# Two-layer hybrid RWKV-7/GLA block on one core: channel-quarter modulation, fused state update, output part in two passes

## The chip, the cores and the metric

One Trainium2 chip; the program runs on 1 core. The metric is the device time of one execution in microseconds (us). Before the change it is 2909.24 us, the median of 3 runs (2906.11 to 2914.11).

## What is computed

```python
for l in range(2):                                  # x_lat: 512 tokens, x_ctx: 256 tokens, 1024 channels
    mod = silu(c) @ ada_w[l] + ada_b[l]             # shift, scale, gate; latent and context rows
    h = rms_norm(x) * norm_mix_pre * (1 + sc_m) + sh_m
    f = h @ w_in[l]                                 # 44 column tiles of 128
    y_rw  = rwkv7(f)   # S_t = S_{t-1}(diag(w_t) - kk_t^T(a_t kk_t)) + v_t^T k_t, both directions, 8 heads
    y_gla = gla(f)     # S = diag(decay) S + k^T v by chunks of 64, both directions, 4 heads
    m = (g_rw * (y_rw @ rw_out) + g_gla * (y_gla @ gla_out)) @ merge_out
    x = x + g_m * rms_norm(m)
    x = x + g_f * rms_norm(square(relu(modulate(x) @ w1)) @ w2)
# context seeds the latent scans; in the last layer only the latent stream goes on after the scans
```

## The kernel before

Activations lie transposed, channels on partitions: 8 tiles of 128 channels, each 768 columns (256 of context "c", 512 latent "l"; GROUPS cuts the latent into "l" and "l2" of 256). Every float32 operand of a large product is split in a high and a low fp32r part, so a weight tile of 128 x 128 costs three matmuls: high by high, high by low, low by high. In the trace these are d<-sh,wh, d<-sl,wh and d<-sh,wl, of 512 or 256 columns. load_w (line 648) fetches a weight in two halves of 256 KB on the SP queue (wr), ScalarE copies the high part (wh), and GpSimd or VectorE subtracts for the low part (wl).

All instructions are recorded by Order and issued from one place (line 541, so the profile names that line for all). A list scheduler (flush, choose) models the five queues with a cost per instruction and issues each engine's instructions in the order of its plan; it is run five times: start, token mixing 0, output part 0, token mixing 1, output part 1. Numbers in CFG and module constants steer it. On the chip each engine then goes through its queue in that order.

- Start (lines 1907 to 1946): the 8 x tiles come in; sum_sq (789) gets the sums of squares per group; scaled multiplies x by the norm. ada_steps (720) takes 32 pieces of the modulation weights (wa, 256 KB each, 8 channel tiles k by 4 quarters u, k outermost), adds each product to acc on VectorE and, after the last, transposes acc and forms MT (shift) and AB (scale). Only then is x modulated (sh high, sl low), and first_tiles (880) multiplies it by column tiles 12, 13 and 14 of w_in, first l, then c, with the weights loaded for each stream.
- Token mixing (897 to 1771): for 6 units (4 of RWKV, 2 of GLA) and 3 groups of 4 chunks, threads of small matmuls are woven with large products as fill (gates, next projections, ada pieces). rw_C (1297) is the sequential part of RWKV: in each of 4 steps a product with the state ZS (c<-ZS,AR), a copy (pre), a product (c<-pre,YI), a copy (ZA), a product (c<-ZA,TK), and the state update on VectorE. There are 2 x 12 x 4 - 8 = 88 such updates; gla_C (1547) has 44 of its own, on GZ.

```python
dve.tensor_tensor(out=gs[hs], in0=pr[hs, :, h], in1=zs[hs, sl, h, :], op=ALU.add)
dve.tensor_tensor(out=nz[hs, ns, h, :], in0=gs[hs], in1=E[hs, sl]..., op=ALU.mult)   # both for h = 0, 1
```

- Output part (1773 to 1897): merge product (weights wmrg, 8 tiles), norm and residual, MLP with 4 blocks of 8 tiles w1 and 8 tiles w2, norm and residual, and in layer 0 the first tiles of layer 1. post_mod (829) is the norm chain of one group: sum_sq of the product, u and x (multiply and residual add), sum_sq of x, then u, sh and sl, the input of the next product. To give PE work meanwhile, held (1809) keeps the last weights on chip (4 of 8 in layer 0, 5 in layer 1, and 3 of w1) and runs through them once for each group of 256 columns; the other tiles go over 512 and 256 columns at once (body). weave (851) sets at which step a group's chain goes on.

Of the kernel before, what the change touches and what calls it, by code (L numbers as in the profile page):

```python
# [53 lines left out]
def constants():  # L54
# [44 lines left out]

CFG = {  # L100
    "nfill": ((2, 2, 0, 2, 2, 0, 2, 2, 0, 2, 2, 0, 2, 1, 1, 0, 0, 0, 0), (2, 3, 0, 2, 2, 1, 2, 2, 0, 2, 2, 0, 1, 0, 0, 1, 0, 0, 0)),
    "nada": ((2,) * 12 + (0,) * 7, (2,) * 8 + (0,) * 11),
# [13 lines left out]
    "oe": ((-1, 1, 2, 9, 10), (-1, 1, 2, 5, 7)),  # L116
    "ch": (0,),
# [19 lines left out]
LATEF = 50e3  # L137


class Order:  # L140
# [7 lines left out]
    def __init__(self, tc):  # L148
        self.tc = tc
        self.nodes = []  # L150
        self.clock = {e: 0.0 for e in ISSUE}
        self.dma = 0.0
        self.flow, self.win, self.sum, self.slow, self.lost = deque(), 0, 0.0, False, 0.0
        self.cfg = None
        self.table = None
        self.alloc = {}
        self.slots = {}
        self.free0 = 0.0
        self.last = {}
        self.end_of = {}  # L160
        self.serial = {}
# [35 lines left out]
    def add(self, key, op, fn, a, k):  # L197
# [61 lines left out]
        if key == "PE":  # L259
            n["kind"] = (n["cfg"], str(lhs.dtype), op, n["w"][0][0].cap_key if n["w"] else None)  # L260
            n["calls"] = 1
            n["fill"] = bool(n["w"]) and str(n["w"][0][0].cap_key).startswith("d1")
# [54 lines left out]
    def flush(self):  # L317
        self.depend()
        ns = self.nodes
        left, members = {}, {}  # L320
        for n in ns:
# [6 lines left out]
            for name, t in ts.items():  # L328
# [9 lines left out]
                elif left[name] == 1:  # L338
                    kk = self.slots[t.cap_key]
                    kk["free"] = [x for x in kk["free"] if x[1] != name]  # L340
        want, cands = {}, {e: [] for e in ISSUE}
# [34 lines left out]
        def choose(e):  # L376
# [15 lines left out]
            best, low = [], None  # L392
            for n in cands[e]:
# [19 lines left out]
            if e == "PE" and self.cold(low):  # L413
                d = [x for x in best if x[0] <= low + tol and x[1]["flow"] >= 0.7 * x[1]["d"]]
                near = d or near
            return min(near, key=lambda x: x[1]["prio"])
# [9 lines left out]
        while done < len(ns):  # L426
# [11 lines left out]
            if e == "DVE" and n["two"] and self.clock["POOL"] > s + 100.0:  # L438
                d += 0.9 * min(d, self.clock["POOL"] - s)
            f = s + d  # L440
            if e == "POOL" and vec is not None and vec["two"] and self.clock["DVE"] > s + 50.0:
                x = 0.9 * min(self.clock["DVE"] - s, d)
# [17 lines left out]
            if e == "SP":  # L460
                self.dma = max(self.dma, s + 1300.0) + n["bytes"] / 200.0
                f = self.dma + 700.0
# [9 lines left out]
            for name, t in n["tiles"].items():  # L472
# [12 lines left out]
                if not left[name]:  # L485
# [63 lines left out]
def hybrid_kernel(ctx: ExitStack, tc: tile.TileContext, A: dict, out: bass.AP):  # L549
# [96 lines left out]
    D0, D1 = One("d0"), One("d1")  # L646

# [141 lines left out]
    def sum_sq(pl, xs, grp, cuts, eng=pool, psp=ops):  # L789
        s, o, n = grp  # L790
        nt = n // 128
        parts = []
        for j in range(KT):
            x = xs[j][:, o:o + n]
            if j in cuts:
                S = pl.tile([P, n], F32, name="S", tag="S", bufs=6)
                act.activation(out=S, in_=x, func=AF.Square)
                parts.append(S)
            else:
                q = pl.tile([P, n], F32, name="q", tag="q", bufs=2)  # L800
                act.activation(out=q, in_=x, func=AF.Square)
                eng.tensor_tensor(out=parts[-1], in0=parts[-1], in1=q, op=ALU.add)
            if j == 5 and cuts is CHAIN:
                yield
        pc = psp.tile([P, 512], F32, name="d", tag="d")
        for i, S in enumerate(parts):
            for t in range(nt):
                mm(pc[:, t:t + 1], S[:, 128 * t:128 * t + 128], ones, start=(i == 0 and t == 0),
                   stop=(i == len(parts) - 1 and t == nt - 1))
# [19 lines left out]
    def post_mod(pl, ms, l, which, grp, xs, store_x, l2, which2, acts):  # L829
        s, o, n = grp  # L830
        si = SI[s]
        bc = yield from sum_sq(pl, ms, grp, CHAIN)
# [10 lines left out]
        bc = yield from sum_sq(pl, xs, grp, PAIRS)  # L843
# [7 lines left out]
    def weave(dd, dw, chains, offs, then=()):  # L851
# [7 lines left out]
        for p in range(max(len(steps), max(at) + 1)):  # L859
            for ch in at.get(p, ()):  # L860
                next(ch, None)
# [35 lines left out]
    def mixer(l, acts, adas, pre, early):  # L897
# [399 lines left out]
        def rw_C(X, gi):  # L1297
# [10 lines left out]
            for st in range(4):  # L1308
                cc = (st, 7 - st)
                sl = slice(st, 8 - st, 7 - 2 * st)  # L1310
                pp = cps.tile([P, 2, 2, 64], F32, name="c", tag="c")
# [14 lines left out]
                if st < 3:  # L1326
                    nz, ns = zs, slice(st + 1, 7 - st, 5 - 2 * st)
                else:
                    nz, ns = nzs, slice(0, 8, 7)
                pr = cps.tile([P, 2, 2, 64], F32, name="c", tag="c")  # L1330
                gs = G([P, 2, 64], "gs", 2)
# [215 lines left out]
        def gla_C(X, gi):  # L1547
# [9 lines left out]
            for st in range(4):  # L1557
# [11 lines left out]
                sl = slice(st, 8 - st, 7 - 2 * st)  # L1569
                nz, ns = (z, slice(st + 1, 7 - st, 5 - 2 * st)) if st < 3 else (nz_, slice(0, 8, 7))  # L1570
                gs = G([P, 2, 128], "Q", 2, name="gs2")
                for h in range(2):
                    hs = HS[h]
                    dve.tensor_tensor(out=gs[hs], in0=pu[hs, st % 2], in1=z[hs, sl, h, :], op=ALU.add)
                    dve.tensor_tensor(out=nz[hs, ns, h, :], in0=gs[hs], in1=E[hs, sl].unsqueeze(2).to_broadcast([64, 2, 128]), op=ALU.mult)
# [197 lines left out]
    def out_mlp(l, last, ya, wo):  # L1773
        full = l == 0
        st = STREAMS if full else STREAMS[:1]
        groups = GROUPS if full else GROUPS[:2]
# [4 lines left out]
        with ExitStack() as mx:  # L1781
# [4 lines left out]
            nt = 4 if full else 5  # L1786
            hslots = [[(hp, t, 8) for t in ("ah", "al", "ah", "al")]] * (nt - 1) + [None]
            bslots = [None] + [[(bp, t, 8) for t in ("bh", "bl", "bh", "bl")]] * 2
# [20 lines left out]
            def held(srcs, acts, evac, ms_, slots):  # L1809
                ws = {}  # L1810

                def one(i, m, g):
                    if m not in ws:
                        ws[m] = load_w(srcs[m], slots[i], PD)
                    evac(m, dense(ws[m], acts(), [g]), [g])

                return [[(lambda i=i, m=m, g=g: one(i, m, g)) for i, m in enumerate(ms_)] for g in groups]
# [22 lines left out]
            xs = []  # L1840
            for j in range(8):
# [180 lines left out]
```

## Time and profile before

| | |
|---|---|
| median of the runs | 2909.24 us |
| profiled execution | 2908.16 us, span 2906.4 us |
| mean granted TensorE clock | 0.961 |
| PE busy / VectorE / ScalarE / GpSimd | 2714.6 / 1635.9 / 1242.9 / 1128.6 us |
| bytes moved | 257.12 MB, mean 88 GB/s |

PE is TensorE, DVE VectorE, ACT ScalarE, POOL GpSimd, SP the queue that issues the transfers. A busy PE is not PE at its peak: the ends of matmuls are modelled, so the pitch from start to start tells more than the duration. A window row gives each engine's busy time in a stretch and its granted clock.

### The profile page before, as it was taken

What the parts mean: (1) busy time and instruction counts of PE and PEld (TensorE: products, weight loads), DVE (VectorE), ACT (ScalarE), POOL (GpSimd) and SP (SyncE); (2) the same over time, 40 slices, a digit from 0 to 9 for tenths busy, and PEclk for the clock granted to TensorE, in tenths of its full rate; (3) what the DMA queues carried; (4) which work ended last, traced back from release to release, by engine and by line L of the source; (5) the groups of instructions that cost most, each with busy time, mean ns of one, the idle gap of its engine ahead of it and who ended that gap; (6) DMA issues with size and microseconds to landing.
All of it is one profiled execution on the core that took longest, in us unless ns stands there. A gap on an engine that the chain in (4) does not pass through costs nothing.

```text
span 2906.4 us, 56280 instructions
## 1 busy us (share of the span) xinstructions
PE 2714.6 (93%) x22616; PEld 2243.8 (77%) x22616; DVE 1635.9 (56%) x3155; ACT 1242.9 (43%) x2542; POOL 1128.6 (39%) x1310
## 2 busy tenths in 40 slices
PE   6999999999988989999999899989988978899998
PEld 4788778778767988888889666767776756888887
DVE  6577888786677251122224538887878787422223
ACT  3555454545552343323133545545444572443332
POOL 2745444542330442223135546444333241533334
PEclk9999999999999989999999899989978999899999
DMA  6422323231225212222222343222301115223332
GB/s 218 130 87 68 106 76 102 81 106 59 83 85 208 83 37 64 64 62 63 65 62 85 109 146 97 74 89 79 98 16 35 40 49 183 78 84 95 95 97 81
DMA packets 137780, 257.12 MB, mean 88 GB/s; under 512 B 15312, under 2 KB 24272, under 8 KB 137520
## 3 DMA queue, kind: packets, MB, share of 16 engines
q1 hardware_dynamic: 137520, 253.53, 28.0%
q8 instruction: 178, 2.92, 0.4%
q14 instruction: 82, 0.67, 0.1%
HBM read 223.45 MB, written 30.02 MB: 87 GB/s over the span
## 4 chain that ended last, share of the span: by engine, by line
PE 54%; DVE 8%; issue 3%; ACT 3%; POOL 3%; DMA 1%; SPq 0%; POOLq 0%; ACTq 0%; DVEq 0%
PE d L541 45%; PE c L541 4%; PE m L541 3%; PE i L541 2%; DMA g<-odr 1%; PE da L541 1%; DVE lw L541 1%; DVE AR L541 1%; POOL S L541 1%; DVE u L541 1%; DVE ZS L541 1%; POOL wl L541 0%; DVE gs L541 0%; DVE BK L541 0%; DVE g L541 0%
## 5 line engine op out<-in xcount | busy, mean ns | idle before, releaser
L541 PE MATMUL d<-sh,wh 128*128 128x512 f32 (+1 forms) x3304 | 1198.4, 363 | 48.0 <-ACT wh L541 19.2
L541 PE MATMUL d<-sh,wl 128*128 128x512 f32 (+1 forms) x3304 | 1144.0, 346 | 12.3 <-POOL wl L541 9.1
L541 PE MATMUL d<-sl,wh 128*128 128x512 f32 (+1 forms) x3304 | 1145.3, 347 | 4.9 <-POOL sl L541 2.8
L541 PEld LDWEIGHTS d<-sh,wh 128*128 128x128 f32 x3304 | 634.0, 192 | 157.7 <-issue 27.4
L541 POOL TENSOR_TENSOR wl<-wr,wh 128x512 fp32r<-128x512 f32 x319 | 427.4, 1342 | 779.6 <-ACT wh L541 715.6
L541 PEld LDWEIGHTS d<-sh,wl 128*128 128x128 f32 x3304 | 633.8, 192 | 95.6 <-POOL wl L541 13.7
L541 PEld LDWEIGHTS d<-sl,wh 128*128 128x128 f32 x3304 | 635.1, 192 | 70.5 <-DVE sl L541 4.8
L541 ACT ACTIVATE wh<-wr 128x512 fp32r<-128x512 f32 x506 | 313.7, 626 | 477.0 <-PE d L541 380.6
L541 DVE TENSOR_TENSOR wl<-wr,wh 128x512 fp32r<-128x512 f32 x187 | 144.3, 777 | 182.1 <-ACT wh L541 177.0
L541 DVE TENSOR_TENSOR t<-t,d 128x256 f32<-128x256 f32 (+1 forms) x102 | 58.2, 572 | 320.4 <-ACT t L541 320.4
L541 POOL TENSOR_TENSOR sl<-t,sh 128x512 fp32r<-128x512 f32 (+2 forms) x73 | 103.1, 1414 | 220.4 <-ACT sh L541 220.4
L541 DVE TENSOR_TENSOR a<-a,d 128x512 f32<-128x512 f32 (+1 forms) x81 | 44.4, 549 | 219.4 <-PE d L541 219.3
L541 ACT ACTIVATE XY<-i 128x512 f16<-128x512 f32 x192 | 109.2, 594 | 108.0 <-PE i L541 106.2
L541 ACT ACTIVATE t<-d 128x256 f32<-128x256 f32 (+1 forms) x102 | 51.4, 506 | 165.2 <-PE d L541 165.1
L541 POOL TENSOR_TENSOR rn<-rn,C 128x2 f32<-128x2 f32 (+2 forms) x41 | 58.8, 1433 | 150.6 <-DVE rn L541 150.2
L541 POOL TENSOR_TENSOR LTL<-AB,LTB 64x512 f16<-64x512 f32 x48 | 63.4, 1322 | 125.3 <-DVE LTB L541 123.5
L541 PE MATMUL da<-wa,SC 128*32 128x128 f32 x1536 | 86.2, 302 | 21.8 <-DMA wa<-in_ada_dram 15.3
L541 POOL TENSOR_TENSOR S<-S,q 128x256 f32<-128x256 f32 x102 | 77.2, 765 | 70.8 <-ACT q L541 69.8
L541 PEld LDWEIGHTS <-XY 64*64 64x64 f16 x1920 | 66.5, 111 | 46.7 <-issue 34.4
L541 DVE TENSOR_TENSOR Q<-i,MK 128x512 f16<-128x512 f32 x120 | 82.6, 689 | 24.2 <-PE i L541 21.4
L541 ACT ACTIVATE f<-d 128x512 f32<-128x512 f32 (+1 forms) x85 | 54.5, 651 | 88.9 <-PE d L541 68.0
L541 PE MATMUL i<-Q,XY 64*64 64x64 f16 x1920 | 84.1, 199 | 8.4 <-DVE Q L541 5.8
(252 smaller groups left out, 4221.5 us busy)
## 6 DMA issues: line engine op xcount, KB each, us to landing
wr<-in_w_dram SPq DMA_DIRECT2D x256, 256.0 KB, 2.7
wa<-in_ada_dram SPq DMA_DIRECT2D x192, 256.0 KB, 2.7
wr<-in_win_dram SPq DMA_DIRECT2D x186, 256.0 KB, 2.9
wr<-in_wout_dram SPq DMA_DIRECT2D x32, 256.0 KB, 3.8
wr<-in_wmrg_dram SPq DMA_DIRECT2D x32, 256.0 KB, 3.1
gdr<-fg SPq DMA_DIRECT2D x20, 384.0 KB, 2.9
gdr<-fg SPq DMA_DIRECT2D x20, 256.0 KB, 2.0
xi<-in_xt_dram SPq DMA_DIRECT2D x8, 384.0 KB, 6.9
```

Of the source, the lines that this page charges most:

```text
L541: ins = fn(*a, **k).ins
```

## The change

1. Start: the modulation weights are taken with the quarter u outermost, each quarter summed in PSUM over its 8 pieces. After each quarter, the two channel tiles j = u and 4 + u are modulated and their part of the three first products (both streams, weights loaded once) is issued.
2. State update: new = E * (product) + E * (old state). ScalarE forms E * old (zse, ze), VectorE does one scalar_tensor_tensor for each direction and head half.
3. Output part: held is replaced by passes: all 8 tiles of wmrg and of the last w2 block go over l (512 columns) and then, loaded again, over c (in layer 1: l, then l2, 256 each); so do the first 3 (layer 1: 5) tiles of w1. The chains of l and l2 start together after the first pass. Sums of squares are formed in two halves, and their PSUM comes from fixed banks.
4. The scheduler gets other costs, other constants for each of its five runs, and other tables of fill.

```diff
-    "nfill": ((2, 2, 0, 2, 2, 0, 2, 2, 0, ...
+    "nfill": ((2, 2, 0, 3, 1, 0, 3, 1, 0, ...
...
-    "oe": ((-1, 1, 2, 9, 10), (-1, 1, 2, 5, 7)),
-    "ch": (0,),
+    "oe": ((-1, 1, 2, 5, 6), (-1, 1, 2, 5, 6)),
+    "ch": (0, 4),
...
+SEG = [
+    dict(AHEAD=20.0, HOLD=8000.0, HYST=0.0, LATE=80000.0, LATEF=80000.0, SLACK=0.0, WARM=0.45),
...
-                n["d"] = 150.0 + 0.87 * c
+                n["d"] = 175.0 + 0.87 * c + (100.0 if any(isinstance(k.get(x), bass.AP) for x in ("bias", "scale")) and c > 64 else 0.0)
...
+    CB = ({"l": D0, "l2": D0, "c": D1}, {"l": D0, "l2": D1})
...
+                if not (gi == NG - 1 and st == 3):
+                    zse = G([P, 2, 64], "zse", 1)
+                    for d in range(2):
+                        for h in range(2):
+                            act.activation(out=zse[HS[h], d], in_=zs[HS[h], cc[d], h, :], func=AF.Copy, scale=E[HS[h], cc[d]:cc[d] + 1])
...
-                for h in range(2):
-                    hs = HS[h]
-                    dve.tensor_tensor(out=gs[hs], in0=pr[hs, :, h], in1=zs[hs, sl, h, :], op=ALU.add)
-                    dve.tensor_tensor(out=nz[hs, ns, h, :], in0=gs[hs], in1=E[hs, sl].unsqueeze(2).to_broadcast([64, 2, 64]), op=ALU.mult)
+                for d in range(2):
+                    for h in range(2):
+                        hs = HS[h]
+                        dve.scalar_tensor_tensor(out=nz[hs, ns[d], h, :], in0=pr[hs, d, h], scalar=E[hs, cc[d]:cc[d] + 1],
+                                                 in1=zse[hs, d], op0=ALU.mult, op1=ALU.add)
...
-            def held(srcs, acts, evac, ms_, slots):
-                ws = {}
...
+            def passes(srcs, acts, evac, ms_):
+                def one(m, g):
+                    evac(m, dense(load_w(srcs[m], None, PD), acts(), [g]), [g])
+
+                return [[(lambda m=m, g=g: one(m, g)) for m in ms_] for g in groups]
...
-        ag = ada_steps(0, 0, ini, "ra", 28)
...
+        for u in range(4):
+            ps = cps.tile([P, 512], F32, name="da", tag="c")[:, 0:128]
+            for k in range(KT):
+                raw = ini.tile([P, 4, 128], F32, name="ra", tag="ra", bufs=26)
...
+                    mm(ps[32 * g:32 * g + 32, :], SC[:, k, :], raw[:, g], start=(k == 0), stop=(k == KT - 1))
...
+            for j in (u, 4 + u):
...
+            for s, o, n in STREAMS:
+                for i, w in enumerate(ws):
...
+                    for q in range(2):
+                        ah, al = acts[4 * q + u]
```

How the order moves, at three places. PE in the start, from the norm to the first large product (da<-wa and da<-ra are the modulation's pieces, da<-C,acc the transpose, d<-sh the projections). Before:

```order
L541 MATMUL d<-C,rn 128x128 x2
L541 MATMUL da<-wa,SC 32x128 x100
L541 MATMUL da<-C,acc 128x128 x4
L541 MATMUL d<-sh,wh 128x512
L541 MATMUL d<-sl,wh 128x512
L541 MATMUL d<-sh,wl 128x512
```

Now:

```order
L566 MATMUL da<-C,acc 128x128
L566 MATMUL da<-ra,SC 32x128 x12
L566 MATMUL d<-C,rn 128x128 x2
L566 MATMUL da<-ra,SC 32x128 x20
L566 MATMUL da<-C,acc 128x128
L566 MATMUL d<-sh,wh 128x512
L566 MATMUL d<-sl,wh 128x512
L566 MATMUL d<-sh,wl 128x512
```

The first projection stood behind all 128 matmuls of the modulation, and now stands behind 64 of them, with the last 64 in two groups of 32 further down among the projections.

VectorE at the first state update of layer 0. Before:

```order
L541 COPY ZA<-c 64x2x64
L541 TENSOR_TENSOR XY<-i,MK 128x8x64
L541 SCALAR_TENSOR_TENSOR lw<-C,lw 128x260
L541 TENSOR_TENSOR gs<-c,ZS 64x128
L541 TENSOR_TENSOR ZS<-gs,E 64x2x64
L541 TENSOR_TENSOR gs<-c,ZS 64x128
L541 TENSOR_TENSOR ZS<-gs,E 64x2x64
L541 SCALAR_TENSOR_TENSOR lw<-C,lw 128x260
```

Now VectorE, and behind it ScalarE in a later step:

```order
L566 COPY ZA<-c 64x2x64
L566 TENSOR_TENSOR XY<-i,MK 128x8x64
L566 SCALAR_TENSOR_TENSOR ZS<-c,E,zse 64x64 x4
L566 SCALAR_TENSOR_TENSOR ta<-ta,kk 128x256
L566 COPY pre<-c 64x128
```

```order
L566 ACTIVATE zse<-ZS,E 64x64 x4
L566 ACTIVATE pre<-c 64x128
L566 ACTIVATE kr<-ta,PX 128x256
L566 ACTIVATE XY<-i 128x512
L566 ACTIVATE ZA<-c 64x2x64
```

Four instructions of 128 columns become four of 64, and in ScalarE's queue four new copies stand right ahead of the copy pre of the next step (so in 83 of the 96 steps of the program).

PE in output part 0 where the second pass of wmrg ends and w1 begins (d<-C,rn spreads a group's norm over the partitions; here the second one of l2):

```order
L566 MATMUL d<-sh,wh 128x256
L566 MATMUL d<-sl,wh 128x256
L566 MATMUL d<-sh,wl 128x256
L566 MATMUL d<-C,rn 128x128 x2
L566 MATMUL d<-C,S 128x1 x2
L566 MATMUL d<-sh,wh 128x512
L566 MATMUL d<-sl,wh 128x512
L566 MATMUL d<-sh,wl 128x512
```

Before, the second norms of l, l2 and c stood apart, each among products of 256 columns; now those of l and l2 both stand ahead of the first product of w1, which takes 512 columns.

## Rows read from the trace of the kernel before

**Rows 1.** Page, part 1: busy time of each engine, its share and instructions

```profile
PE 2714.6 (93%) x22616; PEld 2243.8 (77%) x22616; DVE 1635.9 (56%) x3155; ACT 1242.9 (43%) x2542; POOL 1128.6 (39%) x1310
```

**Rows 2.** Windows: stretch, length, busy us of each engine, clock, DMA share, GB/s

```profile
0.00:81.00 81.00, 54.36 (x435) 37.92 (x436) 49.66 (x127) 32.44 (x65) 23.85 (x24) 0.94 0.62 213
81.00:942.00 861.00, 818.25 (x8663) 664.68 (x8661) 643.54 (x1255) 417.43 (x883) 350.52 (x460) 0.99 0.31 98
942.00:1076.00 134.00, 125.71 (x832) 116.99 (x833) 61.21 (x123) 58.90 (x139) 61.81 (x72) 0.92 0.21 64
...
1519.00:1642.00 123.00, 108.93 (x702) 99.13 (x700) 58.21 (x124) 47.34 (x104) 57.41 (x70) 0.89 0.28 85
1642.00:2454.00 812.00, 733.93 (x7324) 570.89 (x7320) 601.93 (x1156) 402.68 (x846) 335.45 (x439) 0.93 0.27 84
2454.00:2554.00 100.00, 90.60 (x538) 82.40 (x539) 49.61 (x87) 45.18 (x103) 46.27 (x52) 0.83 0.26 80
...
2863.00:2907.00 44.00, 30.83 (x255) 30.11 (x253) 17.47 (x39) 6.59 (x16) 18.01 (x24) 0.88 0.14 49
```

**Rows 3.** Timeline of PE: start us, us, group, [idle before <-releaser]

```profile
27.09 1.23 PE L541 MATMUL d<-C,rn 128*128 128x128 f32 x4
...
49.08 0.79 PE L541 MATMUL d<-sh,wh 128*128 128x512 f32 x1 [1.53 <-ACT sh L541]
...
79.40 0.28 PE L541 MATMUL d<-sh,wh 128*128 128x256 f32 x1
...
80.35 0.28 PE L541 MATMUL d<-sh,wl 128*128 128x256 f32 x1
80.47 0.40 PE L541 MATMUL d<-sh,wh 128*128 128x512 f32 x1
...
81.86 0.39 PE L541 MATMUL d<-sh,wh 128*128 128x512 f32 x1
```

**Rows 4.** Windows of the start: all engines

```profile
20.00:30.00 10.00, 9.52 (x77) 6.02 (x76) 5.29 (x18) 0.89 (x3) 2.11 (x3) 1.00 1.05 386
```

**Rows 5.** Windows of VectorE's instructions on xi alone: busy us (count), clock, DMA

```profile
20.00:49.00 29.00, 8.77 (x24) 0.96 0.76 265
49.00:72.00 23.00, 17.21 (x24) 0.83 0.21 67
```

**Rows 6.** Groups by form: busy us, mean ns of one, idle before

```profile
L541 DVE TENSOR_TENSOR wl<-wr,wh 128x512 fp32r<-128x512 f32 x187 | 144.3, 777 | 182.1 <-ACT wh L541 177.0
L541 DVE TENSOR_TENSOR ZS<-gs,E 64x128 f32<-64x128 f32 x176 | 79.7, 453 | 6.0
L541 DVE TENSOR_TENSOR gs<-c,ZS 64x128 f32<-64x128 f32 x176 | 50.5, 287 | 25.0 <-PE c L541 22.8
L541 DVE TENSOR_TENSOR GZ<-gs,E 64x256 f32<-64x256 f32 x88 | 44.3, 503 | 2.9
L541 DVE TENSOR_TENSOR gs<-c,GZ 64x256 f32<-64x256 f32 x88 | 36.9, 420 | 6.4 <-PE c L541 5.1
```

**Rows 7.** Waits of PE in token mixing 0 (first row) and 1: total, times, longest

```profile
PE c L541 <- DVE ZS L541: 2.1, 6, 0.7
PE c L541 <- DVE ZS L541: 12.8, 12, 2.5
```

**Rows 8.** Groups by form: copies on ScalarE

```profile
L541 ACT ACTIVATE pre<-c 64x128 f32<-64x128 f32 x96 | 25.9, 270 | 103.0 <-PE c L541 79.0 <-DVE pre L541 19.4 <-DVE acc L541 3.3
L541 ACT ACTIVATE sc<-f,PR 128x769 f32<-128x769 f32 x14 | 13.2, 941 | 1.1
L541 ACT ACTIVATE f<-sc 128x769 f32<-128x769 f32 x14 | 11.9, 848 | 15.7 <-DVE sc L541 15.7
```

**Rows 9.** Groups by form: VectorE in the norm chain

```profile
L541 DVE SCALAR_TENSOR_TENSOR u<-a,AB,d 128x256 f32<-128x256 f32 x80 | 35.7, 471 | 10.4 <-PE d L541 9.4 <-POOL x L541 0.9
L541 DVE SCALAR_TENSOR_TENSOR sl<-u,MT,sh 128x256 fp32r<-128x256 f32 x64 | 31.2, 530 | 1.2 <-ACT sh L541 0.9
L541 DVE TENSOR_TENSOR x<-x,u 128x256 f32<-128x256 f32 x40 | 23.3, 583 | 1.2
```

More of the change, by code (lines that the diff above doesn't have):

```diff
@@ L317, in flush @@
     def flush(self):
+        if SEG:
+            globals().update(SEG.pop(0))
         self.depend()
         ns = self.nodes
-        left, members = {}, {}
+        left, parts = {}, {r[0].name for n in ns for r in n["w"] if r[0].dtype == F32R}
+        used = {r[0].name for n in ns for r in n["r"] if n["eng"] == "PE" or r[0].name not in parts}
         for n in ns:
@@ L791, in sum_sq @@
         nt = n // 128
-        parts = []
+        pc = None
         for j in range(KT):
@@ L801, in sum_sq @@
                 act.activation(out=q, in_=x, func=AF.Square)
-                eng.tensor_tensor(out=parts[-1], in0=parts[-1], in1=q, op=ALU.add)
+                eng.tensor_tensor(out=S, in0=S, in1=q, op=ALU.add)
+            if j + 1 in cuts or j == KT - 1:
+                if pc is None:
+                    pc = psp.tile([P, 512], F32, name="d", tag="d")
+                for t in range(nt):
+                    mm(pc[:, t:t + 1], S[:, 128 * t:128 * t + 128], ones, start=(j + 1 == min(cuts[1:], default=KT) and t == 0),
+                       stop=(j == KT - 1 and t == nt - 1))
             if j == 5 and cuts is CHAIN:
                 yield
[L805 to L809, printed above, removed]
         rn = sml.tile([P, 12], F32, name="rn", tag="rn")
@@ L1775, in out_mlp @@
         st = STREAMS if full else STREAMS[:1]
-        groups = GROUPS if full else GROUPS[:2]
+        groups = STREAMS if full else GROUPS[:2]
+        halves = [GROUPS[:2], GROUPS[2:]] if full else [[g] for g in GROUPS[:2]]
+        nf = 3 if full else 5
         o0 = 0 if full else L0
@@ L1839, in out_mlp, with ev_mrg @@
                 mh.append(split(("bh", "bl"), res[0], o0, n0, bp, lo_eng=dve))
+            ms = [acc.tile([P, NT], F32, name="a", tag="a") for _ in range(8)]
+            def ev_mrg(m, ps, sts):
+                for s, o, n in sts:
+                    act.activation(out=ms[m][:, o:o + n], in_=ps[s], func=AF.Copy)
+            wm = [A["wmrg"][l, m] for m in range(8)]
             xs = []
@@ L1844, in out_mlp @@
                 xs.append(x)
-            ms = [acc.tile([P, NT], F32, name="a", tag="a") for _ in range(8)]
-            def ev_mrg(m, ps, sts):
-                for s, o, n in sts:
-                    act.activation(out=ms[m][:, o:o + n], in_=ps[s], func=AF.Copy)
-            wm = [A["wmrg"][l, m] for m in range(8)]
-            body(wm, mh, ev_mrg, range(8 - nt), True)
             for c in range(4):
@@ L1890, in store_x @@
                     sp.dma_start(out=xdr[0][:, j, o:o + n], in_=x[:, o:o + n])
[L1892 to L1894 removed]
+            weave(passes(w2, lambda: hd, ev_o, range(8)), [],
+                  [[post_mod(tp, ac, l, 3, g, xs, store_x, l + 1, 0, None if last else new_h) for g in gs] for gs in halves], CFG["oe"][l],
+                  () if last else ((16, lambda: first_tiles(l + 1, late["h"], pre, "l")), (22, lambda: first_tiles(l + 1, late["h"], pre, "c"))))
             early = {} if last else {8: load_w(A["win"][l + 1, 8], c=0)}
@@ L1927, in hybrid_kernel @@
-        for _ in ag:
-            pass
+        gs = [sum_sq(ini, xs, g, CHAIN, dve, ops) for g in GROUPS]
+        bcs = ini.tile([P, NT], F32, name="bc")
+        for _ in range(3):
+            for i, g in enumerate(gs):
+                try:
+                    next(g)
+                except StopIteration as e:
+                    o, n = GROUPS[i][1:]
+                    act.activation(out=bcs[:, o:o + n], in_=e.value, func=AF.Copy)
+        acts = [alloc_hl(("ah", "al")) for _ in range(8)]
```

146 lines of the change are left out of this document (83 added, 63 removed).

## The prediction

> **What bounds the kernel now.** I read the engines' busy times first [rows 1]: PE is at work in 93% of the span, no other engine in more than 56%. So time can be won where PE waits, and the windows by stage say where that is [rows 2]: in token mixing 0 PE is busy 818.25 of 861 us, but in the start 54.36 of 81, in the first stretch of output part 0 (merge product to the norm of the MLP) 125.71 of 134, in its last 108.93 of 123. Busy time flatters these stretches, because a matmul's end is modelled. I therefore take the pitch, start to start, from the timeline of PE [rows 3]: six 512-column matmuls from 80.47 to 81.86 give 0.232 us each, eight 256-column ones from 79.40 to 80.35 give 0.119. A product of 8 channel tiles and 3 parts costs 24 x 0.232 = 5.57 us over l, 24 x 0.119 = 2.86 over c, 8.42 over both. What a stretch holds at this pitch, against its length, is its excess; that is the working measure for the output part.
>
> - Output 0, first stretch: 8 tiles wmrg and 3 of w1 over both streams, 11 x 8.42 = 92.7; of 134 us 41 are excess.
> - Output 0, last stretch: 8 tiles w2, three first tiles over l and two over c, 8 x 8.42 + 3 x 5.57 + 2 x 2.86 = 89.8; of 123 us 33 are excess.
> - Output 1, first stretch: 8 wmrg and 5 w1 products' worth over l, of which I count 8 x 5.57 + 6 x 2.86 = 61.7; of 100 us 38 are excess.
>
> **The start: -22.** The first projection begins at 49.08 us behind the whole modulation, and the next stage's first matmul at 80.47 [rows 3]. The granted clock is 0.94 on the mean there [rows 2], near the 2.4 GHz level. Afterwards the projections run beside the modulation's pieces, and three things can set the end. The transfers: pieces and weights are about 13.7 MB, which at 386 GB/s [rows 4] are 35.5 us, so they are in well before 58. PE: its products are the same, less than half of the stage. VectorE: the norm's spread stands at 27.09 and takes 1.23 [rows 3], so modulating starts near 28.8; VectorE then has the work on x, 8.77 + 17.21 us [rows 5], and three low parts of weights at 0.777 [rows 6], 28.3 us in all. That ends at 57.1; the last quarter's products add some 1.5. From 80.47 to 58.5 are 22 us. Bounds: -28, if a third of the work on x lies ahead of 28.8 (some of the 24 instructions before 49 do); -12, if PE falls to 1.2 GHz in the gaps between quarters, or VectorE and the last quarter follow one another.
>
> **Output 0, first stretch: -19.** The c pass of wmrg, 8 x 2.86 = 22.9 us, now covers the chains of l and l2, and w1 over l covers that of c. A group's chain on VectorE has 16 u at 0.471, 8 sl at 0.530 and part of the x at 0.583, of which half are GpSimd's [rows 9]: 16 x 0.471 + 4 x 0.583 + 8 x 0.530 = 14.1 us. Two groups and 8 low parts of weights at 0.777 [rows 6] make 34.4; the first product of w1 needs only the first channel, so 7 x 1.0 us come off, and the chain starts 2.5 us after the pass: 30 against the cover of 22.9, a stall of 7. The chain of c, about 22 us with its weights, stands beside 3 x 5.57 = 16.7: a stall of 5. Two sums of squares on the path cost 4 more, first weights 3, the clock (0.92 here [rows 2]) 3. So 22 of the 41 stay. Bounds: -30 (stalls and clock gone), -8 (the chains take the pass twice as long as counted, since three engines share them).
>
> **Output 0, last stretch: -13,** the same chains, with the first tiles over l and c as cover; some 20 of 33 stay. Bounds -24 and -5.
>
> **Output 1, first stretch: -12.** l and l2 are 256 columns each and now go in two passes with 5 tiles of w1. Of the 38, 24 stay: first weights 8, stalls 2 and 6, sums 4, clock 4 (0.83 granted [rows 2]). Two more us are the price of going in 256 columns where 512 went before: 24 x (2 x 0.119 - 0.232) = 0.14 for a tile, 8 to 13 of them. Bounds -20 and -3.
>
> **The tail of output 1: 0.** The last 44 us [rows 2] are the chain of the last group, which has no product behind it and the same length as before.
>
> **The reloaded weights: 0.** 74 halves of 256 KB, 19.4 MB, come in a second time, in stretches where 64 to 85 GB/s move [rows 2], against 386 seen in the start [rows 4]. Over four stretches of together 440 us this adds 44 GB/s. If that cover failed, 19.4 MB at 386 GB/s would be 50 us. The copies for wh (on ScalarE) and the low parts (37 more each on GpSimd and VectorE) go to engines that are busy less than half of these stretches [rows 2].
>
> **Token mixing 0 and 1: -11.** An RWKV update has two pairs of VectorE instructions, 0.287 and 0.453 [rows 6], 2 x 0.740 = 1.48 us. Four of 64 columns take their place. The trace has no such instruction; 0.287 at 128 and 0.420 at 256 columns [rows 6] give 1.04 ns a column, so 0.22 at 64 by the line, and 0.287 if a short one costs as much as one of 128. The update becomes 0.88 to 1.15, a gain of 0.33 to 0.60. One of GLA, 2 x (0.420 + 0.503) = 1.85, becomes 4 x 0.287 = 1.15, a gain of 0.70. Over 88 and 44 updates that is 60 to 84 us of VectorE, but VectorE is not what PE waits for: it is busy 643.54 of 861 us [rows 2], and PE waits for ZS 6 times in token mixing 0, 2.1 us, and 12 times in token mixing 1, 12.8 [rows 7]. I take the 18 waits by 0.60 us: -11. Bounds: -60 (the update is on the path everywhere, the wait named elsewhere), and above nothing by the next point. On ScalarE the change adds 352 copies zse and 176 ze with a pointer as scale. A pre of 64 x 128 takes 0.270; a pointer makes 0.941 out of 0.848, 0.093 more [rows 8]. 528 at 0.27 to 0.363 are 143 to 192 us, on an engine busy 417.43 of 861 and 402.68 of 812 us [rows 2]. They need only the old state, so they can run under the first two products of their step; I cost them at nothing. That cover goes when pre stands right behind them in ScalarE's queue and its product is done: 83 of the 96 steps have that order. Then each step waits up to 4 x 0.363 = 1.45 us.
>
> There the Trainium skill speaks against the change: ScalarE: Activation LUTs, section "Rules for kernel authors", wants a multiply on VectorE and not on ScalarE, and budgets about 0.3 us for an activation with a pointer operand and about 0.83 ns for each element. By it the 528 copies would be an estimated 352 x 0.353 + 176 x 0.406 = 196 us, just past the upper end from the rows, so the sum would stay as it is unless they lie on the path; that is the first rival.
>
> **Sum.** -22 - 19 - 13 - 12 - 11 = -77, against the profiled execution of 2908.16 us (span 2906.4 and 1.8 around it): 2831. The median is 1.1 above that execution, so 2832.
>
> **Rivals.**
> First, the copies land on the path (chance 0.06). Place: ScalarE's queue ahead of pre in each step. Price: an RWKV step pays 1.45 and gets 0.60 back, 88 x 0.85 = 75; one of GLA pays 1.45 and gets 0.70, 44 x 0.75 = 33. Together +108, with -66 from the start and the output part +42: 2951, slower. From about 0.5 us net per update (132 x 0.5 = 66) it eats up the rest. For it: the queue order, and 79.0 us that ScalarE idled ahead of pre for the product c [rows 8], so pre is issued the moment PE is done. Against it: just this idle time, 79.0 over 96 copies, is 0.8 us each in which copies of the old state can run, and PE has fill between the steps. The rule of the page named above would stand beside this rival.
>
> Second, the output part keeps its stalls (0.17). The second loads bring 37 more low parts to both GpSimd and VectorE and 74 copies to ScalarE, all in the stretches where these form the chains; if they stand ahead of the chain's work, the passes only move the wait. Then the start and the mixing remain: -33, 2876. For it: VectorE's 34 us of work against 22.9 of cover. Against it: VectorE and ScalarE are busy 61.21 and 58.90 of the first stretch's 134 us [rows 2], so there is room for 37 x 0.777 = 29 us more in four stretches.
>
> Third, the whole saving of the state update is on the path (0.13): 88 x 0.33 + 44 x 0.70 = 60 in place of 11, so 2783. For it: the recurrence is the one strictly serial part of the mixing, and a wait for c can be a late ZS. Against: PE is busy 818.25 of 861 us there [rows 2].
>
> Fourth, nothing that can be measured (0.04), 2909: the new plan of the mixing gives back what start and output win.
>
> **How the numbers follow.** My forecast has 0.60. Its own bounds, start -28 to -12, output part -74 to -16, mixing 0 to -25, won't all fall on one side: together they allow -127 to -28, and half of the way to each from -77 is 2807 to 2856, the forecast's own range. The range 2775 to 2885 takes in the second and third rivals and leaves out the first, the fourth and some of the forecast's tails, 2 in 10 together. This kernel's measurement can tell 0.3%, 8.7 us, from no change. Slower by more than that is the first rival, 0.06; no difference is the fourth, 0.04; faster is the rest, 0.90.
>
> **What would show it.** Start: a first-tile product before 40 us and the next stage's first matmul at 58 instead of 80. Output part: stretches of some 115, 110 and 90 us for the same products, the wait of PE on sh or sl in two places of 5 to 7 us each, no wait on a transfer. State update: a form of 64 x 64 on VectorE at 0.22 to 0.29, ScalarE's busy time up by 140 to 190 us, waits for ZS halved, both mixing stretches shorter by 2 to 9 us. The forecast is wrong if PE waits for pre in most steps (first rival), if VectorE is late in the output part with wl ahead of u (second), or if the mixing becomes shorter by over 20 us each (third).

## The result and the profile after

The changed kernel takes 2880.11 us (median of 4 runs, 2880.05 to 2886.5) against 2911.3 in the same session: a ratio of 0.990, 95% interval 0.988 to 0.9921. It is faster, as forecast, by 31 us and not by 77. The profiled execution is the longest of its four (2886.5 us, span 2884.7); the other three are 6.4 us shorter, so the trace shows 22 of the 31 us.

Each stage begins with the first matmul that uses its first weight, found by matching PE's order with its timeline. Every stage has the same products before and after. Lengths in us:

| stage | before | after | difference | forecast |
|---|---|---|---|---|
| start | 80.5 | 63.7 | -16.8 | -22 |
| token mixing 0 | 872.8 | 862.0 | -10.8 | |
| output 0, first wmrg to second w1 block | 231.1 | 238.7 | +7.6 | -19 |
| output 0, middle | 335.5 | 335.5 | 0 | 0 |
| output 0, last w2 block and first tiles | 122.1 | 130.0 | +7.9 | -13 |
| token mixing 1 | 818.0 | 806.7 | -11.3 | -11 for both |
| output 1, wmrg and first w1 block | 120.9 | 120.2 | -0.7 | -12 |
| output 1, middle | 265.0 | 265.0 | 0 | 0 |
| output 1, last w2 block and tail | 60.5 | 63.0 | +2.5 | 0 |

The output part lost 17 us in all where 44 were to be won; mixing won 22.

Part 1 of the page of the changed kernel, as [rows 1]:

```profile
PE 2714.0 (94%) x22596; PEld 2249.0 (78%) x22596; DVE 1603.8 (56%) x3154; ACT 1470.5 (51%) x3144; POOL 1172.0 (41%) x1336
```

PE has the same work. ScalarE has 228 us more, from the new copies and 74 more splits. VectorE has 32 us less: the update's groups fell from 211.4 us [rows 6] to 161.0 (below), the low parts rose from 144.3 to 171.5. The windows of the changed kernel at the stages of the table, middle stretches left out (columns as in [rows 2]):

```profile
0.00:63.70 63.70, 47.48 (x444) 39.11 (x444) 40.93 (x88) 28.23 (x59) 19.62 (x24) 1.00 0.70 248
63.70:925.70 862.00, 828.67 (x8713) 674.00 (x8714) 619.04 (x1263) 516.33 (x1155) 349.45 (x459) 0.99 0.32 100
925.70:1164.30 238.60, 225.94 (x1250) 196.69 (x1249) 79.30 (x145) 97.59 (x201) 100.91 (x94) 0.96 0.27 82
1499.80:1629.90 130.10, 114.97 (x603) 100.29 (x602) 63.88 (x128) 55.95 (x118) 67.02 (x72) 0.88 0.35 104
1629.90:2436.50 806.60, 736.25 (x7342) 575.66 (x7341) 576.04 (x1157) 496.46 (x1112) 333.44 (x443) 0.93 0.28 86
```

In the output stretches no engine but PE is busy for much more than half of the time (the most is GpSimd's 67.02 of 130.1 us), and still PE loses time there. One reason shows inside the second pass. PE of the changed kernel in output part 0, pass of wmrg over c:

```profile
986.84 0.28 PE L566 MATMUL d<-sl,wh 128*128 128x256 f32 x1
989.67 0.39 PE L566 MATMUL d<-sh,wl 128*128 128x256 f32 x1 [2.56 <-POOL wl L566]
...
995.04 0.28 PE L566 MATMUL d<-sl,wh 128*128 128x256 f32 x1
996.86 0.58 PE L566 MATMUL d<-sh,wl 128*128 128x256 f32 x1 [1.53 <-POOL wl L566]
997.23 0.41 PE L566 MATMUL d<-sh,wh 128*128 128x256 f32 x1
997.45 0.41 PE L566 MATMUL d<-sl,wh 128*128 128x256 f32 x1
```

PE has the high part and waits for the low part of the same weight. What GpSimd did meanwhile:

```profile
983.90 2.07 POOL L566 TENSOR_TENSOR S<-S,q 128x256 f32<-128x256 f32 x2
985.93 0.72 POOL L566 TENSOR_TENSOR x<-x,u 128x256 f32<-128x256 f32 x1
986.62 1.59 POOL L566 TENSOR_TENSOR S<-S,q 128x256 f32<-128x256 f32 x2
988.17 1.44 POOL L566 TENSOR_TENSOR wl<-wr,wh 128x512 fp32r<-128x512 f32 x1
989.58 0.73 POOL L566 TENSOR_TENSOR x<-x,u 128x256 f32<-128x256 f32 x1
```

It was in the chains of l and l2 (S and x), and wl stood behind five of their instructions. After these gaps the pitch of a 256-column matmul is 0.22 us (997.23 to 997.45) against 0.119 in [rows 3], and the granted clock from 996.8 to 1004.0 is 0.50: PE has dropped from its 2.4 GHz level to 1.2. PE's waits in this second pass (971 to 1016), and below them in that of the last w2 block (1545 to 1601), as in [rows 7]:

```profile
PE d L566 <- POOL wl L566: 4.3, 3, 2.6
PE d L566 <- DVE u L566: 0.9, 1, 0.9
```

```profile
PE d L566 <- ACT sh L566: 6.5, 1, 6.5
PE d L566 <- DVE u L566: 3.9, 2, 2.1
PE d L566 <- POOL wl L566: 2.4, 3, 1.9
```

So the late wl is the main wait in the first of the two. In the second it is the chain's own sh and u that are late.

The start came out near the forecast. VectorE's last piece of modulation, then on PE the first matmul of the last quarter's products, their last one and the next stage's first:

```profile
57.49 1.30 DVE L566 TENSOR_SCALAR xi<-xi,AB,MT 128x256 f32<-128x256 f32 x1 [0.21 <-ACT sh L566]
```

```profile
56.50 0.39 PE L566 MATMUL d<-sh,wh 128*128 128x512 f32 x1
...
62.70 0.28 PE L566 MATMUL d<-sh,wl 128*128 128x256 f32 x1
63.72 0.50 PE L566 MATMUL d<-sh,wh 128*128 128x512 f32 x1 [0.74 <-ACT f L566]
```

For the state update, groups by form:

```profile
L566 ACT ACTIVATE zse<-ZS,E 64x64 f32<-64x64 f32 x352 | 121.3, 345 | 67.2 <-DVE ZS L566 62.7
L566 ACT ACTIVATE ze<-GZ,E 64x128 f32<-64x128 f32 x176 | 70.0, 398 | 11.6 <-DVE GZ L566 7.7
L566 ACT ACTIVATE pre<-c 64x128 f32<-64x128 f32 x96 | 25.7, 268 | 9.6 <-DVE pre L566 5.2 <-PE c L566 2.7
L566 DVE SCALAR_TENSOR_TENSOR ZS<-c,E,zse 64x64 f32<-64x64 f32 x352 | 99.5, 283 | 34.6 <-PE c L566 27.6
L566 DVE SCALAR_TENSOR_TENSOR GZ<-c,E,ze 64x128 f32<-64x128 f32 x176 | 61.5, 349 | 10.6 <-PE c L566 5.1 <-ACT ze L566 0.4
```

The row to look at is pre. Before, ScalarE stood idle 79.0 us ahead of it, waiting for PE's product [rows 8]; now 2.7, and it stands idle 62.7 us ahead of zse, waiting for the old state. ScalarE no longer waits for the product: it comes too late for it. Over the 96 steps pre begins a median 0.04 us after its product's end in the kernel before and 0.82 in the changed one (mean 0.21 and 0.78). It stands directly behind the copies in 67 of the 96 steps, not in 83; in 25 more other instructions of ScalarE stand between.

PE's waits in the recurrence over the whole run, before and after (columns as in [rows 7]):

```profile
PE c L541 <- DVE ZS L541: 14.9, 18, 2.5
PE c L541 <- DVE pre L541: 2.4, 5, 1.3
PE c L541 <- POOL GZ L541: 2.2, 2, 1.7
PE c L541 <- ACT pre L541: 2.0, 2, 1.4
```

```profile
PE c L566 <- DVE GZ L566: 6.5, 9, 1.7
PE c L566 <- ACT pre L566: 5.1, 12, 1.2
PE c L566 <- DVE pre L566: 4.8, 7, 1.3
PE c L566 <- DVE ZS L566: 2.3, 5, 1.2
```

The wait for ZS went, as forecast, by 12.6 us; 5.5 came back as waits for pre and 4.3 as waits for GZ, so 2.8 are left.

### The profile page after: what moved, and what is told of

Same layout as the page of the kernel before. It is cut to its first block, busy times and chain, and to the rows that moved or that the text cites. A ratio compares the mean times of both kernels' runs of the same rounds, so it can differ in the third digit from the quotient of the medians.

```text
span 2884.7 us, 57083 instructions
## 1 busy us (share of the span) xinstructions
PE 2714.0 (94%) x22596; PEld 2249.0 (78%) x22596; DVE 1603.8 (56%) x3154; ACT 1470.5 (51%) x3144; POOL 1172.0 (41%) x1336
## 4 chain that ended last, share of the span: by engine, by line
PE 51%; DVE 7%; ACT 4%; POOL 4%; issue 2%; DMA 1%; SPq 0%; POOLq 0%; ACTq 0%; DVEq 0%
PE d L566 43%; PE c L566 3%; PE m L566 2%; PE i L566 2%; POOL wl L566 1%; POOL S L566 1%; POOL x L566 1%; DVE sl L566 1%; DVE ZS L566 1%; DVE AR L566 1%; DVE u L566 1%; ACT zse L566 1%; PE da L566 1%; DVE GZ L566 0%; ACT f L566 0%
## 5 line engine op out<-in xcount | busy, mean ns | idle before, releaser
L566 POOL TENSOR_TENSOR wl<-wr,wh 128x512 fp32r<-128x512 f32 x356 | 476.0, 1339 | 793.9 <-ACT wh L566 770.6
L566 ACT ACTIVATE wh<-wr 128x512 fp32r<-128x512 f32 x580 | 361.9, 627 | 469.3 <-PE d L566 389.6
L566 DVE TENSOR_TENSOR wl<-wr,wh 128x512 fp32r<-128x512 f32 x224 | 171.5, 770 | 187.0 <-ACT wh L566 178.9
L566 DVE TENSOR_TENSOR t<-t,d 128x512 f32<-128x512 f32 (+1 forms) x101 | 58.2, 576 | 318.2 <-ACT t L566 318.1
L566 ACT ACTIVATE zse<-ZS,E 64x64 f32<-64x64 f32 x352 | 121.3, 345 | 67.2 <-DVE ZS L566 62.7
L566 ACT ACTIVATE XY<-i 128x512 f16<-128x512 f32 x192 | 107.8, 591 | 59.1 <-PE i L566 57.1
L566 ACT ACTIVATE t<-d 128x512 f32<-128x512 f32 (+1 forms) x101 | 51.4, 509 | 161.4 <-PE d L566 161.3
L566 DVE SCALAR_TENSOR_TENSOR ZS<-c,E,zse 64x64 f32<-64x64 f32 x352 | 99.5, 283 | 34.6 <-PE c L566 27.6
L566 POOL TENSOR_TENSOR LTL<-AB,LTB 64x512 f16<-64x512 f32 x48 | 63.9, 1332 | 122.1 <-DVE LTB L566 88.1
```

Of the source, the lines that this page charges most:

```text
L566: ins = fn(*a, **k).ins
```

## The experiments

All differences are to the changed kernel, unless the run starts from the kernel before. "Mixing" gives the two lengths, "output" the stretches of the table: output 0 first, output 0 last, output 1 first. Lengths come from the one profiled execution of each run, times are medians. How far one length can be trusted shows in mixing 0: the changed kernel, held_back, no_reload, keep3, second_dve and second_pool have the same order there, and it took 857.1 to 862.0 us.

**held_back.** out_mlp, sum_sq and post_mod of before.

```diff
-weave(passes(wm, ...), passes(w1, ..., range(nf)), [[post_mod(...) for g in gs] for gs in halves], ...)
+weave(held(wm, ..., hslots), held(w1, ..., range(3), bslots), [[post_mod(...)] for g in groups], ...)
```

> The output part of before (held, chains of l, l2 and c one after the other, sums formed at once, its own weave points) inside the changed kernel; start, state update and the scheduler's costs and constants stay changed. In the changed kernel the stretch from the first wmrg product to the second block of w1 took 238.4 us against 231.4 before, the one from the last w2 block to token mixing 1 130.3 against 122.2. Theory A (the passes cost more than they win): both go back, 7 + 8 us, so 2880 - 15 = 2865. Rival (the new constants of the scheduler or the other stages cause it): both stretches stay at 238 and 130, 2880.

Output 230.2, 121.8, 123.1: both stretches of layer 0 go back to what they were, so the passes with their chains and sums, and not the scheduler's constants, cost the 16 us. The time is 2896.57 all the same, since mixing 1 takes 842.2 us in place of 806.7. That was not foreseen (see held_late).

**no_reload** and **keep3.** no_reload leaves out the loads, high copies and low parts of the second passes of wmrg and the last w2 block: their eight products all take the weights of tile 7, kept from the first pass. keep3 keeps three tiles and loads the other five again.

```diff
 def one(m, g):
-    evac(m, dense(load_w(srcs[m], None, PD), acts(), [g]), [g])
# no_reload, kept = (7,)
+    if g is groups[0] or not kept:
+        w = load_w(srcs[m], hslots if m in kept else None, PD)
+        if m in kept:
+            ws[0] = w
+    else:
+        w = ws[0]
# keep3, kept = (0, 1, 2)
+    w = ws.pop(m) if m in ws else load_w(srcs[m], hslots if m in kept else None, PD)
...
+    evac(m, dense(w, acts(), [g]), [g])
```

> The second pass over wmrg and over the last w2 block loads and splits no weights: all 8 tiles of that pass use tile 7 of the first pass, kept on chip (so these products are computed with the wrong weights; PE's work is the same). Theory A1 (splitting the weights again crowds GpSimd, VectorE and ScalarE while the chains of the norms run there): the 44 us of the second pass in output part 0 go towards 30, likewise in the last stretch, some 5 us in output part 1; 2880 - 30 = 2850. Theory A2 (the chains of l and l2 are too long for a pass whatever the weights do): 2875 to 2880.

> Tiles 0 to 2 of wmrg and of the last w2 block stay on chip from the first pass to the second, the other five are loaded and split again. Theory A1: three eighths of what no_reload wins, about 11 us, 2869. Theory A2: 2880.

no_reload: output 223.0, 114.2, 116.8; 2859.23 us. keep3: 236.3, 117.5, 113.5; 2860.79 us, ratio to before 0.9838 (0.9813 to 0.9864), the lowest median of the kernels that leave nothing out. The second pass of wmrg in output part 0, from its first product to its last, in the changed kernel and then in no_reload:

```profile
970.80:1014.80 44.00, 38.59 (x253) 37.11 (x251) 24.72 (x47) 23.24 (x55) 31.42 (x35) 0.81 0.29 90
```

```profile
965.70:996.30 30.60, 30.46 (x253) 29.83 (x251) 17.18 (x39) 15.20 (x40) 20.53 (x28) 1.00 0.01 1
```

The pass falls from 44.0 to 30.6 us, GpSimd's busy time from 31.4 to 20.5, and the granted clock rises from 0.81 to 1.00. The clock is the larger part: 0.19 of 44.0 us is an estimate of 8 us of lost work, beside 5.2 us of waits for wl and u; together they are about the difference of 13.4. No engine waits for a transfer in this pass of the changed kernel. Without the second loads and splits the passes are better than held (223.0 against 231.1, 114.2 against 122.1), so the idea of the passes is worth some 16 us in layer 0, and loading and splitting again costs it 31. A1 holds; which of the parts left out (load, high copy, low part) costs most is not separated. Of the 31 us the time shows 21, since mixing 1 took 816.0 us there. For keep3 the gain is in other places than expected: 2 us in the first stretch, 12.5 in the last, 6.7 in output 1.

**second_dve** and **second_pool.** Low parts of the second passes on one engine.

```diff
-load_w(srcs[m], None, PD)
+load_w(srcs[m], None, PD if g is groups[0] else (dve, dve))    # second_pool: (pool, pool)
```

> In the second pass over wmrg, the last w2 block and the first w1 tiles both low parts of a weight are formed on VectorE, none on GpSimd (before: one on each). GpSimd then has 1.34 us less for each tile, VectorE 0.77 more. Theory G (GpSimd, 31.5 of 45 us busy in the second pass of output part 0, is the crowded engine, since its sums S and its half of x are links of the chain): the first and last stretch of output part 0 (238.7 and 130.0) get 5 to 10 us shorter each, 2865. Rival V (VectorE is as close): no change within 4 us, or longer.

> In the second passes both low parts of a weight on GpSimd, none on VectorE: 1.34 us more on GpSimd for each tile, 0.77 less on VectorE. With both on VectorE the first and last stretch of output part 0 took 242.9 and 134.7 against 238.7 and 130.0 us. If VectorE alone is the crowded engine: both get 5 us shorter. If GpSimd and VectorE are both links of the chain (what moves to one is missing there): 240 to 250 and 132 to 140.

second_dve: output 242.9, 134.7, 117.0, 2894.39 us; second_pool: 232.9, 128.7, 124.2, 2909.77 us (mixing 1 at 835.3). Moving work to VectorE lengthens layer 0 by 4 and 5 us, moving it to GpSimd shortens it by 6 and 1 and lengthens output 1 by 4. Theory G falls: in second_pool GpSimd is busy for 38.3 of the 41.0 us of the second pass of wmrg, and the pass is 3 us shorter than in the changed kernel. These steps are no larger than what an order alone moves (nudge), so which engine is the narrow one stays open; that the second loads and splits as a whole are too much is shown by no_reload, whose steps are twice as large.

**old_update.** Only the state update goes back.

```diff
-act.activation(out=zse..., scale=E...)  # x4, ahead of pre
-dve.scalar_tensor_tensor(out=nz..., in0=pr..., scalar=E..., in1=zse..., op0=ALU.mult, op1=ALU.add)  # x4
+dve.tensor_tensor(out=gs[hs], in0=pr[hs, :, h], in1=zs[hs, sl, h, :], op=ALU.add)
+dve.tensor_tensor(out=nz[hs, ns, h, :], in0=gs[hs], in1=E[hs, sl]..., op=ALU.mult)
```

> Only the state update as before: add and multiply on VectorE, no copies zse and ze on ScalarE; all else as changed. Token mixing got 10.7 and 12.3 us shorter with the change. Theory A (the update's shorter way does it): mixing is 23 us longer again, 2903. Rival 1 (only the named waits for ZS count): 11 us, 2891. Rival 2 (the tables of fill and the scheduler's constants do it): 2880, and the copies on ScalarE are neither a gain nor a loss.

2888.52 us; mixing 852.9 and 822.2, in sum 6.4 us longer. **keep3_old_update** repeats the pair on keep3:

> Three weights kept on chip and the old state update, all else as changed. The old update cost the changed kernel 8 us (2888.5 against 2880.1) with mixing 9 us shorter in layer 0 and 15 longer in layer 1. If the update matters: 2861 + 8 = 2869. Rival P (both are the order's accidents): 2855 to 2875, with mixing between 850 and 865, 800 and 825.

2864.34 us, mixing 852.1 and 819.5, against 861.5 and 804.8: in sum 5.3 longer. By these pairs the fused update is worth some 6 of mixing's 22 us; layer 0 loses 9 by it, layer 1 wins 15. The pairs are not independent, since mixing 0 has the same order in both, and 6 us are no more than an order alone moves (nudge).

**before_fused** and **before_tables.** One part alone in the kernel before: the update, or the tables nfill and nada.

> The kernel before with the fused state update alone (zse and ze on ScalarE, one scalar_tensor_tensor for each direction and half); start, output part and the scheduler's costs and constants are those of before. Token mixing took 872.8 and 818.0 us there. Theory A (the shorter update is worth some us on the path): both get shorter by 4 to 12 us each, 2895. Rival P (the order that the scheduler happens to find decides, since undoing the update in the changed kernel gave one mixing 9 us less and the other 15 more): the two mixings move by up to 15 us either way, and their sum by less than 8.

> The kernel before with the changed tables of fill and of modulation pieces alone; no other line differs. Without constants and tables the changed kernel's mixing was 36 us longer, without the constants alone 1.5 us longer, so the tables stand for most of it there. Theory T (the tables by themselves shorten mixing): 872.8 and 818.0 us become 15 to 35 us shorter together, 2875 to 2895. Rival (they fit only the changed update and plan): within 10 us of 2908, or slower.

before_fused: 2941.33 us, ratio 1.0106 (1.0089 to 1.0123), mixing 890.9 and 833.3. before_tables: 2927.2 us, ratio 1.0063 (1.0042 to 1.0083), mixing 884.7 and 834.6 in an execution that is 12.6 us over its median. Each of the two alone makes the kernel slower. Theory A and theory T both fall, and so does rival P of before_fused, as the sum of its mixings moved by 33 us. What mixing won comes from neither of them alone. With the old update the changed kernel keeps some 16 of the 22 us, so tables, costs and constants together make most of it; costs and constants alone were not run in the kernel before.

**old_consts** and **old_seg.** The changed kernel with SEG empty; old_consts has the tables of before too.

> The changed kernel without its constants for each of the five runs of the scheduler (those of before for all) and with the tables of fill of before; its cost model stays. Theory: the tables and constants are part of what shortened token mixing; without them mixing is 5 to 20 us longer and the rest within 5 us, 2885 to 2905. If they did nothing: 2880.

> The changed kernel without its constants for each of the five runs of the scheduler; its tables of fill and its cost model stay. Without constants and tables it took 2936 us. If the constants do it: 2920 to 2936; if the tables do it: 2880 to 2895.

old_consts: 2935.75 us, start 69.9, mixing 882.0 and 823.2. old_seg: 2896.08 us, start 69.9, mixing 866.3 and 803.9. The constants give the start 6 us; the tables are worth 35 us of mixing in this plan (882.0 + 823.2 against 866.3 + 803.9), though in the plan of before mixing is 28 us longer with them (before_tables, in the execution that was profiled).

**nudge.** `n["d"] = 180.0 + 0.87 * c` for 175.0.

> The changed kernel, with one constant of the scheduler's cost of a ScalarE instruction at 180 instead of 175 ns: the same instructions in another order. It shows how far an order alone moves the time. Rival P: token mixing 0 and 1 (862.0 and 806.7 us) move by 5 to 20 us each. If the order matters little, both stay within 3 us.

2888.77 us: mixing 857.5 and 810.1, output 246.1, 125.1, 120.6. An order alone moves a stretch by up to 7 us, and the time by 9. The mixings moved by 4.5 and 3.4 us, between what the two theories expected, and 857.5 is within what one order of mixing 0 gives.

**zse_after_pre** and **before_fused_late.** The copies zse wait in the schedule for pre of their own step.

```diff
 act.activation(out=pre[HS[0]], in_=pp[HS[0], :, 0], func=AF.Copy)
+at = len(od.nodes) - 1
+act.activation(out=zse..., scale=E...)
+od.nodes[-1]["after"] = at
...
-n["i"], pre = i, set()
+n["i"], pre = i, {n["after"]} if "after" in n else set()
```

> The changed kernel with the four copies zse of an RWKV step placed behind the copy pre of the same step in ScalarE's queue instead of ahead of it (they are needed only by the update at the step's end). In the changed kernel pre begins a median 0.82 us after its product has ended, 0.04 in the kernel before. Theory Z (the copies delay the recurrence): this lag falls below 0.2 us; token mixing 0 and 1 (862.0 and 806.7 us) get 5 to 20 us shorter each, 2860. Rival P (the delay lies beside fill, and the order decides): the lag falls but each mixing stays within 8 us; 2870 to 2890.

> The kernel before with the fused update, and the copies zse behind pre as in the run above. With the copies ahead of pre the fused update alone made the kernel before 31 us slower (mixing 890.9 and 833.3 against 872.8 and 818.0 us). Theory Z: these 31 us go, and some of the update's own saving shows: 2890 to 2912. Rival P: it stays over 2925.

A step of the changed kernel on the timeline (start us, length us, engine, line, operation):

```profile
160.37 1.20 DVE L566 SCALAR_TENSOR_TENSOR ZS<-c,E,zse 64x64 f32<-64x64 f32 x4
161.43 0.68 PE L566 MATMUL c<-ZS,AR 128*128 128x128 f32 x4
161.60 1.43 ACT L566 ACTIVATE zse<-ZS,E 64x64 f32<-64x64 f32 x4 [1.38 <-DVE ZS L566]
163.05 0.27 ACT L566 ACTIVATE pre<-c 64x128 f32<-64x128 f32 x1
...
166.74 1.19 DVE L566 SCALAR_TENSOR_TENSOR ZS<-c,E,zse 64x64 f32<-64x64 f32 x4 [0.76 <-PE c L566]
```

The same step of zse_after_pre:

```profile
159.91 1.19 DVE L566 SCALAR_TENSOR_TENSOR ZS<-c,E,zse 64x64 f32<-64x64 f32 x4
160.97 0.68 PE L566 MATMUL c<-ZS,AR 128*128 128x128 f32 x4
161.68 0.27 ACT L566 ACTIVATE pre<-c 64x128 f32<-64x128 f32 x1
161.85 1.41 ACT L566 ACTIVATE zse<-ZS,E 64x64 f32<-64x64 f32 x4
...
164.69 1.20 DVE L566 SCALAR_TENSOR_TENSOR ZS<-c,E,zse 64x64 f32<-64x64 f32 x4 [0.35 <-PE c L566]
```

The product ends at 162.11; pre begins at 163.05 behind the copies, and without them at once. From one update to the next are 6.37 us against 4.78. Over all steps the median lag of pre falls from 0.82 to 0.13 us. The time is 2869.48 us, ratio to before 0.9866 (0.9851 to 0.988): mixing 0 stays at 861.9, where PE of the changed kernel is at work in 829 of 862 us; mixing 1 falls to 794.4. In the kernel before, the same edit takes the fused update from 2941.33 to 2921.74 (mixing 882.9 and 820.0): two thirds of the loss went with the copies' place, the rest stays open. **keep3_after_pre** puts both edits together:

> Three weights of the first pass kept on chip (2861 us as measured) and the copies zse behind pre. Theory Z: 2861 less what the run above wins, 2840 to 2855. Rival P: 2855 to 2870.

2867.06 us: mixing 862.9 and 805.9, output 236.0, 123.7, 116.7. The two gains don't add; against keep3 mixing 1 keeps its length and the last stretch of output 0 gives back 6 us. By nudge that is the size of an order's accident.

**held_late.** held_back with the copies behind pre.

> The output part of before and the copies zse behind pre, all else as changed. Output part 0 was 17 us shorter with it (230.2 + 121.8), but mixing 1 took 842 us there against 806.7. If those 35 us are an accident of the order: mixing 1 is 790 to 810 and the time 2845 to 2860. If it comes from what the output part of before leaves to mixing 1: 2880 to 2897.

2867.7 us, output 232.3, 122.3, 118.8, and mixing 1 at 807.5. That is 35 us less than in held_back, but the edit also moves the copies, and behind the passes the mixing with late copies took 794.4 us (zse_after_pre), 13 less than here. Mixing 1 has another order in each of these runs. So the 35 us are no fixed price of the old output part; whether all of them are an accident of the order stays open, and the time lies between what the two theories expected.

## Why the prediction was wrong

- **Start, -22: right in kind.** It measured -16.8, inside its bounds. VectorE ends the modulation at 58.79, forecast 57.1. The mis-sized term is what comes behind: "the last quarter's products add some 1.5". They end at 62.98 (62.70 + 0.28), 4.2 us later. A quarter's products are 18 x 0.232 + 18 x 0.119 = 6.3 us; the last quarter's run from 56.50 without a gap, and PE was at work without a gap from 51.50 on, with the third quarter's. So at the end PE's queue of products set the time, and not VectorE.
- **Output part, -44: the step that failed.** It measured +17. First, the excess was too large: the stretch from 942 to 1076 began with 11 us of products of wout (wmrg begins at 953.2), which I counted as empty time. From 953.2 to 1184.4 stand 24 tiles of 8.42 us, 202.1, in 231.1 us: 29 us in all, in place of 41. In output part 1, too, wmrg begins 6 us into the stretch that I took. Second, and decisive, "The reloaded weights: 0 [...] go to engines that are busy less than half of these stretches". That share was an average over the stretch. In the pass itself GpSimd is busy 31.4 of 44.0 us, wl stands behind the chains, PE waits and its clock falls to 0.81. no_reload, without these loads and splits, takes 31 us off layer 0, so the term put at 0 cost 31; which engine makes it so dear stays open (second_dve, second_pool). The transfers were not it, since no engine waits for one in that pass. ([rows 2] has 401 us for the four stretches, where I wrote 440; by that the added rate is 48 GB/s.) It was the second rival, with a chance of 0.17 and 2876 us, in another form: its sign was wl ahead of u on VectorE, and here wl stands behind the chains on GpSimd. The output part came out worse than that rival had it, +17 in place of 0. That the time of 2880.11 us is still near 2876 is luck, since mixing won 11 us more than forecast.
- **Mixing, -11: right in its named wait, wrong in the rest.** The wait for ZS fell by 12.6 us, but waits for pre and GZ took 9.8 of it back. Mixing as a whole won 22, of which the update has some 6 by two pairs of runs, no more than an order alone moves, and the rest came with the scheduler's tables, costs and constants, for which the sum has no term. The form for ZS took 283 ns, the upper of my two values, and the one for GZ 349, where I had 287; VectorE's saving is 50 us where I had 60 to 84.
- **The copies, "I cost them at nothing":** they were not free. In before_fused pre begins a median 0.76 us after its product (0.04 before) and mixing is 33 us longer; with the copies behind pre the lag is 0.10 and 21 of the 33 us are gone (before_fused_late). So the first rival's mechanism was real, at a third of its price of 108 us, and in the changed kernel other gains of mixing hid it. How much of a step's lag reaches the end stays open: zse_after_pre takes a median 0.69 us out of each of 88 steps, 61 us, and mixing becomes 12 us shorter. The argument against it ("0.8 us each in which copies of the old state can run") had the idle time right, but four copies take 1.38.
- **Prices.** zse 345 and ze 398 ns. My rows gave 270 to 363, and ze lies above. The Trainium skill (ScalarE: Activation LUTs, section "Rules for kernel authors") gives about 0.3 us and 0.83 ns an element, an estimate of 353 and 406; the traces agree within 3%. Its advice to multiply on VectorE agrees with before_fused; the two pairs with the old update, whose mixing is 5 to 6 us longer, speak against it in this plan, as far as so little can be told from the effect of an order.
- **The tail, 0:** +2.5. The last w2 block went in two passes there too, with a second load of its weights, which I had left out; with the output part of before (held_back) the stretch takes 60.8 us, as before.

## What to carry to other kernels

Judge a "free" engine by its busy time inside the window where the new work falls, and by what it does first there, not by its share of a long stretch: GpSimd's 42% of the stretch was 71% of the pass. A high share alone doesn't yet name the narrow engine: with more work on GpSimd (second_pool) the same pass was 3 us shorter. Count the clock with the waits: in the second pass the lower clock cost more than the waits did. A helper copy that needs only old data still costs when it stands in an in-order queue ahead of the critical copy; look whether that queue's idle time ahead of the critical copy was longer than the helpers. Where a scheduler decides the order, change one constant that shouldn't matter and see what moves before a few us are given to a cause, and compare stages whose order did not change to see what one execution is worth.

## What the runs showed that was not expected

Orders of the same mixing 1 differ by up to 38 us: 803.9 (old_seg) to 842.2 (held_back). Two parts that each slow the kernel before by 31 and 16 us (before_fused, before_tables) stand together in a kernel whose mixing is 22 us shorter. The GpSimd add S took 838 ns on the mean in the changed kernel, 763 in no_reload and 765 in the kernel before.
